# The order of VectorE's work in the up-projection of a hybrid encoder block

## The chip, the cores and the metric

The kernel runs on one core of a Trainium2 chip. The metric is the device time of one execution in microseconds. Five engines work side by side, each through its own list of instructions: TensorE (PE; its weight loads are PEld) multiplies matrices, VectorE (DVE), ScalarE (ACT) and GpSimd (POOL) work elementwise, and SyncE (SP) issues the DMAs between the chip's memory and the on-chip buffers. An instruction waits at the head of its engine's list until its inputs are there and its output's buffer is free, and everything behind it on that engine waits too.

## The reference

One encoder layer for 2048 frames of 1024 channels. The part that matters here is the second sub-layer:

```python
h2 = modulate(rms_norm(x, g_norm2[l]), shift2, scale2)
u = causal_depthwise_conv(h2 @ w_up[l], w_conv[l], b_conv[l])
val, gte = jnp.split(u, 2, axis=-1)
x = x + (1 + gate2[:, None, :]) * ((val * jax.nn.silu(gte)) @ w_down[l])
```

`w_up` is 1024 x 5632, so val and gte have 2816 columns each; the convolution over frames has three terms, from the frame itself and the two before it. All values are 32-bit floats.

## The kernel before

**Tiling.** The up-projection works through two halves of 1024 frames each, and in each half through 22 blocks of 128 columns of val with the same 128 of gte: `for n in range(2 * NF)`, 44 iterations, `half, f = divmod(n, NF)`. A product of 2 x 2 blocks is done with seven block products instead of eight (Strassen's scheme in Winograd's form), for which sums of the blocks are needed: of the inputs h2 (`h2[0]` to `h2[6]`), of the weights and of the results. Each 32-bit operand is split in two parts, a high one (a copy by ScalarE, L1185) and the rest (a subtraction by POOL or VectorE, L1186), and each block product is 4 x 3 matmuls with 128x512 results (`product`, L1257).

**An iteration.** The results lie in two tiles in TensorE's accumulators, `val` (v; halves a and b) and `gate` (g; halves c_ and d_). TensorE takes the products in a fixed order: 1 into b, 2 into d_, 3 into c_, product 0 of the following iteration into its a, then 4 into a, 5 into b, 6 into c_. Product 0 to 2 use the weight tiles `wua`, 3 to 6 `wub`. Between them VectorE adds (L1261): u2 = b + p1, where p1 is ScalarE's copy of a (L1457); b = d_ + u2, which is the row `v<-g,u` of the profile and is called v below; u3 = c_ + u2; and d_ = d_ + u3, the row `g<-g,u`, called g. ScalarE copies u3 into c_ (L1476), called the copy c. Products 4 and 5 write into v and so wait for v; product 6 waits for g.

**After the products.** `conv` forms the convolution: ScalarE writes the first term from v into cval (L1326, the tap), VectorE adds two more (L1334, L1336) and keeps the last two frames for the second half (halo, L1339); `gate_step` does the same with g into cgate, then silu on ScalarE (L1354) and the multiplication on VectorE (L1355). For an odd f, two blocks are then a pair, and four sums of their halves (gate sums, L1181 and L1366) go with the blocks to memory (`hid_s`, L1347) for the down-projection, which works in the same scheme. `gate_step` is a generator: its steps are done inside the next iteration (`before`).

**Weights.** `make_up` (first half) loads four weight blocks of the next iteration, forms four weight sums on VectorE (s1 = a21 + a22, s2 = s1 - a11, s3 = a11 - a21, s4 = a12 - s2, L1181), splits all seven and stores the sums (`wu_s`); `again_up` (second half) loads them from there. Both are generators too (`made`), stepped between the products. The tiles `ring` are a shared pool of 128x512 buffers for all loads and sums. In iterations 20 to 22 the splits of h2 for the second half come in as well (`swap`, `load_h2`; tiles `h_i_k` in an engine's order, `h` in the profile).

**What sets the order.** Inside the loop TensorE is held to the order of the program (`in_order(("PE",))`). The lists of the other engines are made by a scheduler, which takes from the program's instructions by its own costs and priorities, so there the program's order is one input among others.

Of the kernel before, what the change touches and what calls it, by code (L numbers as in the profile page):

```python
# [26 lines left out]
NF = DFF // P  # L27
# [20 lines left out]
def hybrid_block(ctx, tc, x, c, w_ada, b_ada, g1, w_in, w_fg2, b_fg2, g_gla, w_out, g2,  # L48
# [1124 lines left out]
    def raw(src):  # L1173
        t_ = ring.tile([P, CH], F, name="ring")
        if src is not None:
            dma.dma_start(out=t_ if len(src.shape) == 2 else t_.rearrange("p (k n) -> p k n", k=src.shape[1]), in_=src)
        return t_

    def combine(a, b, op):
        t_ = raw(None)  # L1180
        dve.tensor_tensor(out=t_, in0=a, in1=b, op=op)  # L1181
        return t_
# [17 lines left out]
    def up_block(f, i):  # L1200
        return w_upk[:, KH * (i % 2):KH * (i % 2) + KH, (NF * (i // 2) + f) * P:(NF * (i // 2) + f + 1) * P]

    def put_up(src, eng, res):
        res.append(parts(in_turn(wua if len(res) < 3 else wub[0], 6, [P, 2, CH], R), src, eng))

    def make_up(f, res):

        a11, a12, a21, a22 = (raw(up_block(f, i)) for i in range(4))

        def keep(i, t_):  # L1210
            dma.dma_start(out=wu_s[f][i], in_=t_)

        yield
        put_up(a11, pool, res)
        s1 = combine(a21, a22, ALU.add)
        s2 = combine(s1, a11, ALU.subtract)
        put_up(s2, pool, res)
        put_up(s1, pool, res)
        keep(0, s1)
        yield  # L1220
        s3 = combine(a11, a21, ALU.subtract)
        s4 = combine(a12, s2, ALU.subtract)
        keep(1, s2)
        put_up(s3, pool, res)
        keep(2, s3)
        yield
        put_up(a12, pool, res)
        yield
        put_up(s4, pool, res)
        keep(3, s4)  # L1230
        put_up(a22, pool, res)
        yield

    def again_up(f, res):

        a11, s2, s1 = raw(up_block(f, 0)), raw(wu_s[f][1]), raw(wu_s[f][0])
        yield
        put_up(a11, pool, res)
        s3, a12 = raw(wu_s[f][2]), raw(up_block(f, 1))
        put_up(s2, pool, res)  # L1240
        put_up(s1, pool, res)
        yield
        s4, a22 = raw(wu_s[f][3]), raw(up_block(f, 3))
        put_up(s3, pool, res)
        yield
        put_up(a12, pool, res)
        yield
        put_up(s4, pool, res)
        put_up(a22, pool, res)
        yield  # L1250
# [9 lines left out]
    def add(res, ps, other):  # L1260
        dve.tensor_tensor(out=res, in0=ps, in1=other, op=ALU.add)  # L1261
# [8 lines left out]
    for i in range(3):  # L1270
        for k in range(KH):
            load_h2(0, i, k, dve if (i + k) % 2 else pool)
        if i == 0:
            next(made)
    rest = []
    accs_o = iter([lambda: pools["o"].tile([P, CH], F, name="o"), lambda: ps_z.tile([P, CH], F, name="z"),
# [72 lines left out]
    def gate_step(half, f, cval, gate):  # L1349


        cgate = conv(NF + f, gate, "cgate", half)
        yield
        act.activation(out=cgate, in_=cgate, func=AF.Silu)  # L1354
        dve.tensor_tensor(out=cval, in0=cval, in1=cgate, op=ALU.mult)  # L1355
        q = f // 2
        if f % 2 == 0:
            store_hid(half, q, 0, cval[:, :CH])
            held_val[q] = cval
        else:  # L1360
            (a11, a21), (a12, a22) = ((t_[:, :CH], t_[:, CH:]) for t_ in (held_val.pop(q), cval))
            store_hid(half, q, 1, a12)
            store_hid(half, q, 2, a22)
            s1 = combine(a21, a22, ALU.add)
            s2 = combine(s1, a11, ALU.subtract)
            dve.tensor_tensor(out=a21, in0=a11, in1=a21, op=ALU.subtract)  # L1366
            s4 = combine(a12, s2, ALU.subtract)
            for o, t_ in ((3, s1), (4, s2), (5, a21), (6, s4)):
                store_hid(half, q, o, t_)
        yield  # L1370
# [64 lines left out]
    ordered.enter_context(in_order(("PE",)))  # L1435
    for n in range(2 * NF):
        half, f = divmod(n, NF)
        w, w_next = w_next, []
        s = n % 2
        val = val_next  # L1440
# [10 lines left out]
        def swap(i, now=None):  # L1451
            if half == 0 and (f == NF - 1 if now is None else now):
                for k in range(KH):
                    load_h2(1, i, k, pool if k % 2 else dve)
# [5 lines left out]
            halo_bias()  # L1460
        if n:
            product(b, 1, w, True)
        next(made, None)
        swap(1)
        next(before, None)
        product(d_, 2, w, True)
        add(u2, b, p1)
        next(made, None)
        swap(2)
        product(c_, 3, w, True)  # L1470
        next(made, None)
        swap(3)
        add(b, d_, u2)
        u3 = cv.tile([P, CH], F, name="u3", tag="p1", bufs=1)
        add(u3, c_, u2)
        act.activation(out=c_, in_=u3, func=AF.Copy)  # L1476
        add(d_, d_, u3)
        if n == 2 * NF - 1:
            next_down()
        if n + 1 < 2 * NF:  # L1480
            val_next = ps_u[2 * (1 - s)].tile([P, HT], F, name="v")
            product(val_next[:, 0:CH], 0, w_next, True)
            swap(0, f == NF - 2)
        next(made, None)
        product(a, 4, w, False)
        swap(4)
        if n == 2 * NF - 1:
# [12 lines left out]
        if n in MW:  # L1500
            make_wd(MW.index(n))
        before = gate_step(half, f, cval, gate)
    ordered.close()
    for _ in before:
        pass
# [179 lines left out]
```

## Time and profile before

| | us |
|---|---|
| median of 3 runs | 2674.64 |
| lowest, highest run | 2670.0, 2682.25 |
| profiled execution, its own time | 2680.58 |
| span of its trace | 2678.9 |
| PE busy | 2527.3 (94%) |
| DVE, ACT, POOL busy | 1704.7, 1321.9, 1284.0 |

The profiled execution lies at the upper end of the runs. The span is from the first to the last instruction of the trace. The up-projection's loop takes the span from about 1327 to 2231 us; the mean granted TensorE clock over the whole span is 0.984 of full speed. Busy shares of the whole span say little about one loop: TensorE is busy nearly everywhere, and what matters in the loop is for which other engine it waits.

### The profile page before, as it was taken

To read this page: it belongs to the slowest core of one execution; us is meant where nothing else is said; L and a number is where in the kernel's file an instruction comes from. 1 tells how busy PE (TensorE), PEld (TensorE's weight loads), DVE (VectorE), ACT (ScalarE), POOL (GpSimd) and SP (SyncE) were. 2 spreads that over 40 slices of the span, in tenths; PEclk is the share of its full clock that TensorE was granted. 3 is DMA by queue.
4 is the path that set the end of the run, shared out by engine and by line. 5 is a ranking of instruction groups with operands and counts; after the bars stand their busy time and mean duration, and the time that the engine had idled before them with its cause. 6 is when DMAs were issued, how large, how long until landed. Compare 5 with 4: busy or idle time off the path is not lost. (4 is left out here: it accounts for less than half of the span.)

```text
span 2678.9 us, 36699 instructions
## 1 busy us (share of the span) xinstructions
PE 2527.3 (94%) x12118; PEld 2066.3 (77%) x12118; DVE 1704.7 (64%) x2335; ACT 1321.9 (49%) x2416; POOL 1284.0 (48%) x1100
## 2 busy tenths in 40 slices
PE   5899999999899999999979999989999999999996
PEld 5788888888677777777768778778887877888885
DVE  6535652254988999999566666784554557454668
ACT  4523234232877788888434444454445444333343
POOL 2202122121755556776546556477556553252446
PEclk9999999999999999999989999999999999999998
DMA  8657954576855454554745555576556656544472
GB/s 286 191 173 249 290 170 141 154 241 185 266 185 170 129 149 147 160 164 127 240 139 184 189 174 183 162 243 224 196 174 204 205 181 233 164 142 130 165 273 77
DMA packets 420558, 499.47 MB, mean 186 GB/s; under 512 B 38270, under 2 KB 262796, under 8 KB 418320
## 3 DMA queue, kind: packets, MB, share of 16 engines
q1 hardware_dynamic: 420368, 497.12, 58.6%
q8 instruction: 96, 1.57, 0.3%
q14 instruction: 94, 0.77, 0.1%
HBM read 330.81 MB, written 166.20 MB: 186 GB/s over the span
## 5 line engine op out<-in xcount | busy, mean ns | idle before, releaser
L1009 POOL TENSOR_TENSOR bt<-bt,om 128x512 f32<-128x512 f32 (+2 forms) x320 | 314.2, 986 | 220.1 <-DVE om L1007 122.8
L1186 POOL TENSOR_TENSOR wub<-ring,wub 128x512 fp32r<-128x512 f32 x176 | 239.7, 1366 | 299.4 <-ACT wub L1185 296.7
L1257 PE MATMUL v<-h,wub 128*128 128x512 f32 x1056 | 259.3, 403 | 27.1 <-DVE v L1261 27.0
L1257 PE MATMUL v<-h,wua 128*128 128x512 f32 x1056 | 262.4, 397 | 8.5 <-POOL wua L1186 5.4
L1257 PEld LDWEIGHTS v<-h,wub 128*128 128x128 f32 x1056 | 204.1, 195 | 78.5 <-DVE v L1261 29.7
L1257 PE MATMUL g<-h,wub 128*128 128x512 f32 x1056 | 254.3, 390 | 0.0
L1007 DVE TENSOR_TENSOR_SCAN om<-sg,om,zero 128x513 f32<-128x513 f32 x189 | 240.5, 1272 | 16.0 <-ACT sg L1001 14.8
L1257 PEld LDWEIGHTS v<-h,wua 128*128 128x128 f32 x1056 | 200.9, 191 | 55.4 <-POOL wua L1186 6.6
L1257 PEld LDWEIGHTS g<-h,wub 128*128 128x128 f32 x1056 | 198.2, 188 | 41.9 <-DVE g L1261 0.3
L1651 PE MATMUL d<-h,wub 128*128 128x512 f32 x924 | 222.9, 391 | 0.0
L70 PE MATMUL tr<-ident,bt 128*128 128x128 f32 x1120 | 179.9, 277 | 37.8 <-DVE al L131 24.6
L1404 POOL TENSOR_TENSOR h<-h,h 128x512 fp32r<-128x512 f32 x77 | 116.5, 1516 | 194.7 <-ACT h L1403 173.4
L131 DVE TENSOR_TENSOR al<-tr,ah 128x512 fp32r<-128x512 f32 (+1 forms) x320 | 192.9, 603 | 19.4 <-ACT ah L130 18.6
L1186 POOL TENSOR_TENSOR wua<-ring,wua 128x512 fp32r<-128x512 f32 x132 | 192.1, 1467 | 24.5 <-ACT wua L1185 23.9
L287 POOL TENSOR_TENSOR wr<-wst,wr 128x1024 fp32r<-128x1024 f32 x28 | 71.0, 2540 | 275.0 <-ACT wr L286 275.0
L1651 PEld LDWEIGHTS d<-h,wub 128*128 128x128 f32 x924 | 173.5, 188 | 37.6
L1334 DVE SCALAR_TENSOR_TENSOR cval<-v,conv_w,cval 128x1023 f32<-128x1023 f32 x44 | 56.4, 1282 | 228.6 <-ACT cval L1326 220.0
L130 ACT ACTIVATE ah<-tr 128x512 fp32r<-128x512 f32 (+1 forms) x320 | 179.9, 562 | 26.2 <-PE tr L70 25.6
L70 PEld LDWEIGHTS tr<-ident,bt 128*128 128x128 f32 x1120 | 126.6, 140 | 85.0 <-DVE al L131 35.4
L1002 ACT ACTIVATE bt<-z 128x512 f32<-128x512 f32 (+2 forms) x320 | 174.0, 544 | 0.0
L401 PE MATMUL mm<-wr,hh 128*128 128x512 f32 (+1 forms) x448 | 170.0, 379 | 3.3 <-DVE vt L131 2.0
L403 PE MATMUL mm<-wr,hl 128*128 128x512 f32 (+1 forms) x448 | 168.2, 375 | 0.0
(311 smaller groups left out, 5995.7 us busy)
## 6 DMA issues: line engine op xcount, KB each, us to landing
ring<-in_w_up_dram SPq DMA_DIRECT2D x154, 256.0 KB, 4.9
ring<-hid_s SPq DMA_DIRECT2D x154, 256.0 KB, 4.3
wst<-in_w_in_dram SPq DMA_DIRECT2D x45, 512.0 KB, 7.5
wu_s<-ring SPq DMA_DIRECT2D x88, 256.0 KB, 2.4
hid_s<-cval SPq DMA_DIRECT2D x88, 256.0 KB, 2.4
ring<-wu_s SPq DMA_DIRECT2D x88, 256.0 KB, 5.1
kt<-k_hl SPq DMA_DIRECT2D x80, 256.0 KB, 3.2
vt<-v_hl SPq DMA_DIRECT2D x80, 256.0 KB, 3.3
```

What stands on the lines that cost most here:

```text
L70: pe.transpose(out=o, in_=i, identity=ident)
L130: act.activation(out=hi, in_=ps, func=AF.Copy)
L131: dve.tensor_tensor(out=lo, in0=ps, in1=f32(hi), op=ALU.subtract)
L401: pe.matmul(out=ps[:, :n], lhsT=hh[:, k, sl], rhs=wh, start=k == 0, stop=False)
L403: pe.matmul(out=ps[:, :n], lhsT=hl[:, k, sl], rhs=wh, start=False, stop=k == KD - 1)
L1002: act.activation(out=b1, in_=z[:, :w], func=AF.Sigmoid, scale=0.125)
L1007: dve.tensor_tensor_scan(out=om[:, 0:n_][:, ::-1], data0=beta[:, 0:n_][:, ::-1], data1=zero[0][:, 0:1].broadcast_to([P, n_]), initial=firs ...
L1009: pool.tensor_tensor(out=b1, in0=b1, in1=om[:, 1:w + 1], op=ALU.mult)
L1186: eng.tensor_tensor(out=t_[:, 1], in0=src, in1=f32(t_[:, 0]), op=ALU.subtract)
L1257: pe.matmul(out=ps, lhsT=lhsT, rhs=rhs, start=begin and k == 0 and m == 0, stop=k == KH - 1 and m == 2, skip_group_check=not begin)
L1404: pin(eng.tensor_tensor(out=t_[:, 1], in0=src, in1=f32(t_[:, 0]), op=ALU.subtract))
L1651: pin(pe.matmul(out=ps, lhsT=hd[:, l_, tsl], rhs=w[:, r_], start=begin and q == 0 and m == 0, stop=q == NQ2 - 1 and m == 2, skip_group_che ...
```

## The change

Three things are altered, all in the up-projection. VectorE is held to the order of the program, too, in iterations 2 to 19 and 24 to 43 (`ordered_v`). The program's order is rewritten: v is added ahead of product 3, the generators' steps are cut anew, so that in each iteration they come in turns, with `gate_step` split ahead of and behind the multiplication, and a weight sum s1 ahead of it. And `make_up` stores each weight sum where it is made. No instruction is added or taken away. L1355, L1366, L1457 and L1476 of before are L1356, L1368, L1462 and L1481 in the changed kernel.

```diff
@@ make_up
         put_up(a11, pool, res)
         s1 = combine(a21, a22, ALU.add)
+        keep(0, s1)
+        yield
         s2 = combine(s1, a11, ALU.subtract)
+        keep(1, s2)
         put_up(s2, pool, res)
         put_up(s1, pool, res)
-        keep(0, s1)
         yield
         s3 = combine(a11, a21, ALU.subtract)
+        keep(2, s3)
+        put_up(s3, pool, res)
+        put_up(a12, pool, res)
+        yield
         s4 = combine(a12, s2, ALU.subtract)
-        keep(1, s2)
-        put_up(s3, pool, res)
-        keep(2, s3)
-        yield
-        put_up(a12, pool, res)
-        yield
+        keep(3, s4)
         put_up(s4, pool, res)
-        keep(3, s4)
         put_up(a22, pool, res)
         yield
@@ again_up
         put_up(a11, pool, res)
+        yield
         s3, a12 = raw(wu_s[f][2]), raw(up_block(f, 1))
         put_up(s2, pool, res)
         put_up(s1, pool, res)
         yield
         s4, a22 = raw(wu_s[f][3]), raw(up_block(f, 3))
         put_up(s3, pool, res)
-        yield
         put_up(a12, pool, res)
@@ ahead of the loop
-        if i == 0:
+        if i < 2:
             next(made)
@@ gate_step
         act.activation(out=cgate, in_=cgate, func=AF.Silu)
+        yield
         dve.tensor_tensor(out=cval, in0=cval, in1=cgate, op=ALU.mult)
+        yield
         q = f // 2
@@ the loop
     for n in range(2 * NF):
         half, f = divmod(n, NF)
+        ordered_v = ExitStack()
+        if 2 <= n < NF - 2 or n >= NF + 2:
+            ordered_v.enter_context(in_order(("DVE",)))
...
         if n:
             product(b, 1, w, True)
+        next(before, None)
         next(made, None)
+        next(before, None)
         swap(1)
-        next(before, None)
         product(d_, 2, w, True)
         add(u2, b, p1)
+        add(b, d_, u2)
         next(made, None)
         swap(2)
         product(c_, 3, w, True)
-        next(made, None)
         swap(3)
-        add(b, d_, u2)
         u3 = cv.tile([P, CH], F, name="u3", tag="p1", bufs=1)
         add(u3, c_, u2)
         act.activation(out=c_, in_=u3, func=AF.Copy)
         add(d_, d_, u3)
+        next(made, None)
...
         next(made, None)
+        next(before, None)
         product(a, 4, w, False)
...
         before = gate_step(half, f, cval, gate)
+        ordered_v.close()
```

**VectorE in iteration 16**, an even one of the first half. `ring<-ring` are weight sums, `ring<-cval`, `ring<-ring,cval`, `cval<-cval` and `ring<-cval,ring` the gate sums, `u_16718<-v,p_16717` is u2 and the second u is u3. Before:

```order
L1334 SCALAR_TENSOR_TENSOR cgate<-g,conv_w,cgate 128x1023
L1261 TENSOR_TENSOR u_16718<-v,p_16717 128x512
L1336 SCALAR_TENSOR_TENSOR cgate<-g,conv_w,cgate 128x1022
L1339 COPY halo<-g 128x2
L1355 TENSOR_TENSOR cval<-cval,cgate 128x1024
L1181 TENSOR_TENSOR ring<-cval 128x512
L1181 TENSOR_TENSOR ring<-ring,cval 128x512
L1366 TENSOR_TENSOR cval<-cval 128x512
L1261 TENSOR_TENSOR v<-g,u_16718 128x512
L1261 TENSOR_TENSOR u_16804<-g,u_16718 128x512
L1181 TENSOR_TENSOR ring<-cval,ring 128x512
L1181 TENSOR_TENSOR ring<-ring 128x512 x2
```

VectorE in the same iteration of the changed kernel, from the end of its convolution:

```order
L1339 COPY halo<-g 128x2
L1181 TENSOR_TENSOR ring<-ring 128x512
L1356 TENSOR_TENSOR cval<-cval,cgate 128x1024
L1261 TENSOR_TENSOR u_16718<-v,p_16717 128x512
L1261 TENSOR_TENSOR v<-g,u_16718 128x512
L1181 TENSOR_TENSOR ring<-ring 128x512
L1261 TENSOR_TENSOR u_16780<-g,u_16718 128x512
L1261 TENSOR_TENSOR g<-g,u_16780 128x512
L1181 TENSOR_TENSOR ring<-ring 128x512 x2
L1181 TENSOR_TENSOR ring<-cval 128x512
L1181 TENSOR_TENSOR ring<-ring,cval 128x512
L1368 TENSOR_TENSOR cval<-cval 128x512
```

The four gate sums went from ahead of v and u3 to behind g; the weight sum s1 came ahead of the multiplication, and u2 behind it.

**SyncE in the second half**, at the stores of the pair q = 7 (iteration 38; `wu_s_3_201` is s4 of a following iteration, `in_w_up_dram` a weight block, `wd_s` are sums for the down-projection). Before:

```order
L1347 DMA hid_s_0_119<-cval 128x512
L1176 DMA ring<-in_w_up_dram 128x4x128
L1382 DMA wd_s_127<-ring 128x512
L1382 DMA wd_s_129<-ring 128x512
L1347 DMA hid_s_1_120<-cval 128x512
L1347 DMA hid_s_2_121<-cval 128x512
L1347 DMA hid_s_3_122<-ring 128x512
L1347 DMA hid_s_4_123<-ring 128x512
L1176 DMA ring<-wu_s_3_201 128x512
L1347 DMA hid_s_5_124<-cval 128x512
L1347 DMA hid_s_6_125<-ring 128x512
L1176 DMA ring<-in_w_up_dram 128x4x128 x2
```

SyncE at the same pair in the changed kernel:

```order
L1347 DMA hid_s_0_119<-cval 128x512
L1176 DMA ring<-in_w_up_dram 128x4x128
L1176 DMA ring<-wu_s_3_201 128x512
L1176 DMA ring<-in_w_up_dram 128x4x128
L1384 DMA wd_s_127<-ring 128x512
L1384 DMA wd_s_129<-ring 128x512
L1347 DMA hid_s_1_120<-cval 128x512
L1347 DMA hid_s_2_121<-cval 128x512
L1347 DMA hid_s_3_122<-ring 128x512
L1347 DMA hid_s_4_123<-ring 128x512
L1176 DMA ring<-in_w_up_dram 128x4x128
L1347 DMA hid_s_5_124<-cval 128x512
```

The loads of s4 and of one weight block moved ahead of the stores of the gate sums.

**ScalarE in iteration 21**, where VectorE is not held to the program's order. `h_i_k` are copies of h2 for the second half, `p_17795` is p1 of iteration 22. Before:

```order
L1185 ACTIVATE h_1_2_17575<-ring 128x512
L1354 ACTIVATE cgate<-cgate 128x1024
L1185 ACTIVATE h_1_3_17580<-ring 128x512
L1185 ACTIVATE h_2_0_17608<-ring 128x512
L1185 ACTIVATE wub_17681<-ring 128x512
L1185 ACTIVATE h_2_1_17613<-ring 128x512
L1185 ACTIVATE h_2_2_17618<-ring 128x512
L1476 ACTIVATE g<-u_17664 128x512
L1185 ACTIVATE h_2_3_17623<-ring 128x512
L1185 ACTIVATE h_3_0_17643<-ring 128x512
L1457 ACTIVATE p_17795<-v 128x512
```

ScalarE at the same place in the changed kernel:

```order
L1185 ACTIVATE h_2_1_17606<-ring 128x512
L1185 ACTIVATE h_2_2_17611<-ring 128x512
L1185 ACTIVATE h_2_3_17616<-ring 128x512
L1354 ACTIVATE cgate<-cgate 128x1024
L1185 ACTIVATE h_3_0_17633<-ring 128x512
L1185 ACTIVATE h_3_1_17638<-ring 128x512
L1185 ACTIVATE h_3_2_17643<-ring 128x512
L1185 ACTIVATE h_3_3_17648<-ring 128x512
L1185 ACTIVATE wub_17680<-ring 128x512
L1481 ACTIVATE g<-u_17653 128x512
L1462 ACTIVATE p_17795<-v 128x512
```

silu moved behind the copies h_1_3 and h_2_0 to h_2_3, and the copy c behind h_3_0 to h_3_3 and a weight copy.

## Rows read from the trace of the kernel before

**Rows 1.** Busy table of line L1257's instructions by stretch of the loop, TensorE.

```profile
core 0: us, PE busy (x) PEld busy (x), PEclk, DMA share, GB/s
1630.39:1649.54 19.15, 19.15 (x86) 15.77 (x85) 1.00 0.50 165
1327.14:1391.95 64.81, 44.91 (x169) 35.01 (x168) 0.82 0.51 158
1391.95:1749.68 357.73, 349.20 (x1514) 285.44 (x1513) 0.99 0.55 180
1749.68:1820.12 70.44, 62.68 (x253) 50.25 (x252) 0.93 0.75 244
1839.27:2210.84 371.57, 366.09 (x1597) 298.92 (x1596) 1.00 0.59 194
2210.84:2231.14 20.30, 18.47 (x73) 14.39 (x71) 0.92 0.46 153
```

**Rows 2.** PE's waits, 1324 to 2231: total us, times, longest us.

```profile
PE v L1257 <- DVE v L1261: 27.0, 15, 4.4
...
PE v L1257 <- POOL wua L1186: 5.4, 2, 3.0
PE v L1257 <- ACT wua L1185: 3.1, 1, 3.1
```

**Rows 3.** Timeline of PE, iteration 16: start, us, instruction [idle before <- releaser].

```profile
1682.36 7.32 PE L1257 MATMUL v<-h,wub 128*128 128x512 f32 x24 [2.54 <-DVE v L1261]
```

**Rows 4.** Timeline of DVE, iteration 16.

```profile
1668.53 1.14 DVE L1181 TENSOR_TENSOR ring<-ring 128x512 f32<-128x512 f32 x1 [1.82 <-DMA t_s<-ring]
1671.47 1.28 DVE L1334 SCALAR_TENSOR_TENSOR cval<-v,conv_w,cval 128x1023 f32<-128x1023 f32 x1 [1.79 <-ACT cval L1326]
...
1678.30 1.23 DVE L1355 TENSOR_TENSOR cval<-cval,cgate 128x1024 f32<-128x1024 f32 x1 [1.12 <-ACT cgate L1354]
1679.61 0.69 DVE L1181 TENSOR_TENSOR ring<-cval 128x512 f32<-128x512 f32 x1
...
1681.61 0.69 DVE L1261 TENSOR_TENSOR v<-g,u 128x512 f32<-128x512 f32 x1
```

**Rows 5.** Timeline of ACT, iteration 16.

```profile
1669.71 0.63 ACT L1185 ACTIVATE wua<-ring 128x512 fp32r<-128x512 f32 x1 [1.81 <-DVE ring L1181]
1670.24 1.19 ACT L1326 ACTIVATE cval<-v,conv_b,conv_w 128x1024 f32<-128x1024 f32 x1
```

**Rows 6.** Timeline of ACT, iteration 33.

```profile
2013.67 0.63 ACT L1185 ACTIVATE wub<-ring 128x512 fp32r<-128x512 f32 x1 [3.76 <-DMA ring<-in_w_up_dram]
...
2014.95 1.19 ACT L1326 ACTIVATE cval<-v,conv_b,conv_w 128x1022 f32<-128x1022 f32 x1
...
2022.45 0.63 ACT L1185 ACTIVATE wua<-ring 128x512 fp32r<-128x512 f32 x1 [2.17 <-DMA ring<-in_w_up_dram]
```

**Rows 7.** Line L1181, 1391 to 2211: count, duration ns min/median/max.

```profile
L1181 DVE TENSOR_TENSOR ring<-ring x74: 674/692/1794, 1403.1 to 1764.9; 128x512 f32<-128x512 f32 x74
```

**Rows 8.** Timeline of ACT ahead of iteration 14.

```profile
1627.87 1.21 ACT L1326 ACTIVATE cval<-v,conv_b,conv_w 128x1024 f32<-128x1024 f32 x1 [0.76 <-PE v L1257]
```

**Rows 9.** Timeline of DVE, iteration 21.

```profile
1778.58 3.53 DVE L1186 TENSOR_TENSOR h<-ring,h 128x512 fp32r<-128x512 f32 x2
...
1784.25 0.69 DVE L1261 TENSOR_TENSOR v<-g,u 128x512 f32<-128x512 f32 x1
```

**Rows 10.** Timeline of POOL, iterations 21 and 22.

```profile
1793.81 11.26 POOL L1186 TENSOR_TENSOR h<-ring,h 128x512 fp32r<-128x512 f32 x7
```

**Rows 11.** Timeline of DVE, iteration 0.

```profile
1357.58 0.69 DVE L1261 TENSOR_TENSOR u<-v,p 128x512 f32<-128x512 f32 x1 [1.92 <-ACT p L1457]
...
1361.99 0.69 DVE L1181 TENSOR_TENSOR ring<-ring 128x512 f32<-128x512 f32 x1 [2.40 <-DMA ring<-in_w_up_dram]
...
1363.20 4.09 DVE L1181 TENSOR_TENSOR ring<-ring 128x512 f32<-128x512 f32 x3
```

**Rows 12.** Timeline of PE, iterations 0 and 1.

```profile
1366.10 2.88 PE L1257 MATMUL g<-h,wub 128*128 128x512 f32 x12
...
1382.03 7.37 PE L1257 MATMUL v<-h,wub 128*128 128x512 f32 x24 [2.07 <-DVE v L1261]
```

More of the change, by code (lines that the diff above doesn't have):

```diff
@@ L1215, in make_up @@
         s1 = combine(a21, a22, ALU.add)
+        keep(0, s1)
+        yield
         s2 = combine(s1, a11, ALU.subtract)
+        keep(1, s2)
         put_up(s2, pool, res)
         put_up(s1, pool, res)
-        keep(0, s1)
         yield
         s3 = combine(a11, a21, ALU.subtract)
-        s4 = combine(a12, s2, ALU.subtract)
-        keep(1, s2)
+        keep(2, s3)
         put_up(s3, pool, res)
-        keep(2, s3)
-        yield
         put_up(a12, pool, res)
         yield
+        s4 = combine(a12, s2, ALU.subtract)
+        keep(3, s4)
         put_up(s4, pool, res)
-        keep(3, s4)
         put_up(a22, pool, res)
```

## The prediction

> **What bounds the kernel now.** I read the table of stretches first [rows 1]. An iteration in which nothing waits takes 19.15 us, and TensorE is busy for all of it at the full clock: seven products, of 2.74 us each. So the up-projection can only gain what its 44 iterations take above that. Dividing the stretches: iterations 2 to 19 take 357.73 us where 18 x 19.15 = 344.70 would do, so 13.0 are lost; 20 to 22 take 70.44 instead of 57.45, 13.0 lost; 24 to 42 take 371.57 instead of 363.85, 7.7 lost; 0 and 1 take 64.81 instead of 38.30, 26.5 lost; the last, which has six products, 20.30 instead of 16.42, 3.9 lost. Together 64 of 2680.58 us.
>
> Next, what ended these waits [rows 2]: of 35.5 us of waiting in the products, 27.0 in 15 waits are `v <- DVE v L1261`, VectorE's sum b + d + u2, on which product 4 starts. The other two rows belong to iteration 0, and one wait, the longest on POOL, to iteration 22. Where a wait is long, the granted clock is lower as well: 0.99 in iterations 2 to 19, 0.93 in 20 to 22, and 1.00 in 24 to 42, whose waits are under 2 us [rows 1]. So a long wait costs more than its own length.
>
> Then one such wait, iteration 16 (it begins at 1668.68). On PE, product 4 starts at 1682.36 after 2.54 idle [rows 3], so its inputs from TensorE were ready at 1679.82. VectorE finished v at 1681.61 + 0.69 = 1682.30 [rows 4]. Going back on VectorE: three sums of gate products stand in front of v (1679.61 to 1681.61, 2.0 us); the multiplication before them waited for ScalarE's silu; the whole chain began late, at 1671.47, because the tap (the first term of the convolution, on ScalarE) began at 1670.24. The tap stood behind a weight copy which at 1669.71 waited 1.81 us for a weight sum [rows 5], and this sum ran on VectorE at 1668.53, as early as the scheduler could put it, after 1.82 us of waiting for a DMA [rows 4]. From the tap's start to v's end it is 1682.30 - 1670.24 = 12.06 us. v is due 11.1 us after the iteration's start, so any tap later than about 0.95 us ahead of the start makes PE wait.
>
> The second half of the loop has no weight sums; there the tap is late for a load. In iteration 33 (from 2013.68) a weight copy waited 3.76 us for in_w_up and the tap came at 2014.95, 1.27 after the start; later another copy, waiting 2.17 us for a load, stood ahead of silu [rows 6].
>
> **The change part by part.** No instruction is added or removed; all is order.
>
> *Gate sums behind v (even iterations of both halves, as far as VectorE is held to program order).* Three sums leave the path to v: 0.69 + 0.69 + 0.68 by their rows, 2.0 us by their starts [rows 4]. The u2 sum, 0.68, moves from between the convolution's steps to behind the multiplication and is neutral. One weight sum, s1, comes ahead of the multiplication, but there VectorE sat idle 1.12 us waiting for silu [rows 4], and a sum takes 0.69 in the median [rows 7]: it is hidden, and costs up to 0.7 if stretched to its worst, 1.794. So the tap-to-v time falls to 10.0 us and tolerates a tap up to 1.1 us after the start.
>
> *Weight sums in program order.* Their copies on ScalarE then stand behind the tap and silu instead of ahead of them, so the tap no longer waits for sums. In an undisturbed iteration the tap begins 2.5 us ahead of the start (14: 1627.87 for 1630.39) [rows 8]; from there v is ready 3.5 us early. Even if every tap stayed as late as now, iteration 16 would end v at 1680.30 instead of 1682.30 and wait 0.5. The gate sums and the last weight sums now follow g. Product 3 ends 8.2 us after the start, and u3, the copy c and g, some 0.7 each, bring g to 10.3; six sums of 0.69 bring VectorE to 14.5, and the next convolution begins 1.2 us after its tap [rows 4, 5], at 19.15 - 2.5 + 1.2 = 17.9: covered by 3.4 us.
>
> *The second half.* Three sums leave the path in its even iterations, where nothing was lost anyway; in the odd ones silu stands ahead of the copies that wait for loads, which takes about 0.6 off iteration 33, the copy's own 0.63 (its wait for the load ran beside VectorE's convolution) [rows 6]. The larger part is SyncE: s4's and a22's loads are issued ahead of the stores of the gate sums and not behind them. How much earlier they land no row shows. The bounds are 0, if something else than the stores holds the loads, and 3.76, the whole wait [rows 6]. I take 1.5, nearer the lower, which puts iteration 33's tap where the shorter chain no longer makes PE wait; with nothing from it, 3 of the 7.7 us would remain.
>
> Sum for iterations 2 to 19 and 24 to 42: 13.0 + 7.7 lost now, 2 left (bounds 1 and 4, or 9 if a new wait of 0.5 us came in every second iteration): **-19**.
>
> *Iterations 20 to 22, where VectorE stays with the scheduler.* There v moves ahead of the multiplication in all three. Iteration 20 has the same three sums ahead of v and loses that part. In 21 v ran at 1784.25, behind two splits of h (3.53 us, stretched) and the multiplication [rows 9]; one more split of up to 1.8 and no multiplication stand ahead of it now, so v comes some 2 us earlier; but silu goes behind eight copies of h, and the copy c behind three more, so that the last product of the iteration may wait up to 2 us for g. In 22 PE waits 3.05 us for POOL's first split of a11, behind seven splits of h (11.26 us) [rows 2, 10]; one of these, 1.6 us, now goes behind it: about 1.4 remains. I leave 2.5 in iteration 21, 2.5 in 22 (wait and clock) and 1.5 for a late tap in 20 or 21: 13.0 becomes 6.5, **-6.5** (from -11 to +4).
>
> *The start and the end.* In iteration 0 the copy p no longer stands behind a weight copy; VectorE waited 1.92 us for it at u2, and up to that is taken off PE's longest wait, of 4.4 us [rows 2, 11]. But u3 and g now follow four weight sums, the first of which waits for its load until 1361.99 [rows 11]. These take 4 x 0.69 = 2.8 us at least, and 4.8 by the row of three (4.09) plus 0.69; u3, the copy c and g add 2, so g ends at 1366.8 to 1368.8. Product 6 needs it; it began at 1366.10 [rows 12] and would now begin 1.9 earlier, at 1364.2: a new wait of 2.6 to 4.6 against the 1.9 won, +0.7 to +2.7. Iteration 1 loses the sums ahead of its v, which stands ahead of the multiplication; the wait for v there was 2.07 us [rows 12], and with the lower clock behind it up to 4.0 are gone. A long new wait in 0 lowers the clock as well, so I take 0 for the two: bounds -4 and +4. Iteration 43 has the same sums in another order: 0.
>
> Total: -19 - 6.5 = -25.5 us on the profiled execution of 2680.58, so 2655; the profiled run lies 5.9 us above the median of the runs, so against 2674.64 it is **2649**. A measurement of this kernel can tell about 0.5% from no change, 13 us.
>
> **A rule against it.** The sums that read two SBUF tensors take 0.674 us at best, 0.692 in the median and 1.794 at worst [rows 7]; the long ones lie beside POOL's splits. The addition that reads PSUM took 0.69 in iteration 16 and in 21, where POOL was busy [rows 4, 9]. The Trainium skill, SBUF — State Buffer, section Who interferes with whom, says that a VectorE instruction with two SBUF inputs and a GpSimd instruction reading SBUF exclude each other for the whole instruction; the trace agrees with it, by the 1.794 against 0.674. By that rule the gathered sums would each wait for a split.
>
> **The rivals.** *Port:* six sums in a row, each at 1.79 instead of 0.69, end 6.6 us later, at 21 us instead of 14.5, which is past the next convolution's 17.9 by 3.2. With v now 3.5 us early that costs nothing in most iterations; where the tap was late anyway, up to 1 us in each of 18: -7 in all, 2668. For it speaks the maximum, against it the median. *The waits keep their place:* the loads set the tap, not the sums, and the loads come no earlier, or stand behind gate stores that now come 3 us later; half of both gains goes: -13, 2662. For it speak iterations of the second half, which have no sums and are late all the same. *The turn gives back:* silu and c behind copies of h, and g late in 21 and 22, so that 20 to 22 lose 19 instead of 13: -19 + 6 = -13, 2662. *Slower:* VectorE in program order waits at s1, ahead of the multiplication, u2 and v. If the loads of a21 and a22 come later than 7.8 us after the iteration's start (s1, multiplication, u2 and v take 3.3 us together, of 11.1), PE waits for the rest. At 2.5 us too late in each of 18 iterations 45 us are lost where 13 are now, less the 5.7 and 6.5 of the other stretches: +20, 2694. Against it: in iteration 16 a sum of this kind ran at 1668.53, before the iteration began [rows 4], 8 us ahead of that point. That the order isn't what the change says can be ruled out: it is read off above.
>
> **How the numbers follow.** Forecast 2649 (2640 to 2660): 0.60. Waits keep their place, 2662: 0.17. Turn gives back, 2662: 0.08. Port, 2668: 0.08. Slower, 2694: 0.07. Up to 2667 this holds over 0.8, so the range is 2640 to 2667. 0.5% faster lies at 2661.3: the forecast with a part of the cases around 2662 gives 0.67; within 0.5% 0.26; slower 0.07.
>
> **What would show it.** Right: waits `v <- DVE v` of under 2 us in all in iterations 2 to 19 and 24 to 42, stretches of about 345 and 366 us, gate sums behind g, the tap ahead of the iteration's start. In 20 to 22 about 64 us. Wrong: VectorE idle before a weight sum for a DMA, with PE waiting behind it; iterations of the second half that keep their late taps; `g <- DVE g` as a new wait in iterations 0, 21 or 22.

## The result

The changed kernel takes 2864.07 us in the median of 6 runs (2860.17 to 2868.32), the kernel before 2680.05 in as many; the ratio is 1.0674, 95% interval 1.0644 to 1.0704. It is slower by 184 us where some 25 us less were forecast, and lies far outside the range.

TensorE's waits in the loop of the changed kernel tell where (engine, line, what it waited for: us, times, longest), to be read beside [rows 2]:

```profile
PE g L1257 <- DVE v L1261: 153.9, 44, 15.5
PE tr L70 <- DVE ht L894: 9.1, 1, 9.1
```

All the waits of [rows 2] are gone, those for v before product 4 too. In their place there is one kind: a product into the gate's tile g waits for v, 44 times, once in every iteration. The products that write g with `wub` weights are 3 and 6. Iteration 16 (it begins at 1726.63) shows which one, and how. TensorE and then VectorE, as in [rows 3, 4]:

```profile
1729.39 2.88 PE L1257 MATMUL g<-h,wua 128*128 128x512 f32 x12
1734.55 4.61 PE L1257 MATMUL g<-h,wub 128*128 128x512 f32 x12 [2.28 <-DVE v L1261]
```

```profile
1725.50 1.28 DVE L1334 SCALAR_TENSOR_TENSOR cval<-v,conv_w,cval 128x1023 f32<-128x1023 f32 x1 [6.33 <-ACT cval L1326]
...
1730.66 1.09 DVE L1181 TENSOR_TENSOR ring<-ring 128x512 f32<-128x512 f32 x1
1731.87 1.23 DVE L1356 TENSOR_TENSOR cval<-cval,cgate 128x1024 f32<-128x1024 f32 x1
1733.01 0.68 DVE L1261 TENSOR_TENSOR u<-v,p 128x512 f32<-128x512 f32 x1
1733.80 0.70 DVE L1261 TENSOR_TENSOR v<-g,u 128x512 f32<-128x512 f32 x1
...
1739.20 0.69 DVE L1261 TENSOR_TENSOR u<-g,u 128x512 f32<-128x512 f32 x1 [4.11 <-PE g L1257]
```

Product 2 begins at 1729.39. Product 3 begins at 1734.55, in the moment in which v ends (1733.80 + 0.70 = 1734.50), and ran slowly (4.61 us where 2.88 is the usual row; the granted clock over it was 0.63). VectorE itself is on its plan: the tap is early, s1 runs while ScalarE does silu, and v ends 7.87 us after the iteration's start, where the prediction's steps give about 7.6. But TensorE now needs it 5.5 us after the start and no longer at 11. So VectorE waits for product 3 afterwards (4.11 us before u3), and TensorE and VectorE take turns.

The table of stretches, to be read beside [rows 1] (us, PE busy, PEld busy, clock, DMA): iterations 0 and 1, 2 to 19, 20 to 22, 24 to 42, and 43:

```profile
1328.58:1397.34 68.76, 41.51 (x169) 33.43 (x168) 0.80 0.47 143
1397.34:1819.02 421.68, 372.20 (x1513) 299.24 (x1512) 0.94 0.46 152
1819.02:1896.30 77.28, 63.79 (x253) 51.16 (x252) 0.89 0.74 238
1916.52:2390.85 474.33, 403.17 (x1598) 323.20 (x1597) 0.91 0.45 151
2390.85:2412.05 21.20, 18.44 (x73) 14.38 (x71) 0.92 0.41 145
```

The stretches held to VectorE's order, 421.68 and 474.33 us instead of 357.73 and 371.57, hold 167 of the 181 us between the two spans. Only part of it is waiting: the products' waits grew from 35.5 to 153.9, by 118; PE's busy time in the five stretches grew by 58 (899.1 instead of 841.4), the same matmuls at a granted clock of 0.94 and 0.91 in the two long stretches instead of 0.99 and 1.00; and the wait in tr, transposes that lie between products in iteration 0, grew by 3.

### The profile page after: what moved, and what is told of

The parts are those of the page before. It is cut to its first block, busy times and chain, and to the rows that moved or that the text cites. A ratio compares the mean times of both kernels' runs of the same rounds, so it can differ in the third digit from the quotient of the medians.

```text
span 2859.9 us, 36776 instructions
## 1 busy us (share of the span) xinstructions
PE 2586.6 (90%) x12118; PEld 2105.2 (74%) x12118; DVE 1718.6 (60%) x2335; ACT 1330.4 (47%) x2416; POOL 1285.0 (45%) x1100
## 5 line engine op out<-in xcount | busy, mean ns | idle before, releaser
L1257 PE MATMUL g<-h,wub 128*128 128x512 f32 x1056 | 324.0, 467 | 153.9 <-DVE v L1261 153.9
L1257 PEld LDWEIGHTS g<-h,wub 128*128 128x128 f32 x1056 | 239.2, 231 | 226.5 <-DVE v L1261 108.4
L1257 PE MATMUL v<-h,wua 128*128 128x512 f32 x1056 | 259.0, 394 | 0.0
L1257 PE MATMUL v<-h,wub 128*128 128x512 f32 x1056 | 247.4, 390 | 0.0
L1257 PEld LDWEIGHTS v<-h,wua 128*128 128x128 f32 x1056 | 202.5, 192 | 46.6
L1186 POOL TENSOR_TENSOR wua<-ring,wua 128x512 fp32r<-128x512 f32 x132 | 185.3, 1412 | 106.3 <-ACT wua L1185 100.0
L1257 PEld LDWEIGHTS v<-h,wub 128*128 128x128 f32 x1056 | 198.7, 188 | 41.8
L70 PE MATMUL tr<-ident,bt 128*128 128x128 f32 x1120 | 180.2, 277 | 38.1 <-DVE al L131 24.4
L1185 ACT ACTIVATE wub<-ring 128x512 fp32r<-128x512 f32 x176 | 109.0, 630 | 221.2 <-PE g L1257 127.0
L70 PEld LDWEIGHTS tr<-ident,bt 128*128 128x128 f32 x1120 | 126.7, 140 | 85.6 <-DVE al L131 35.5
```

Source lines behind the costliest of these rows:

```text
L70: pe.transpose(out=o, in_=i, identity=ident)
L1185: act.activation(out=t_[:, 0], in_=src, func=AF.Copy)
L1186: eng.tensor_tensor(out=t_[:, 1], in0=src, in1=f32(t_[:, 0]), op=ALU.subtract)
L1257: pe.matmul(out=ps, lhsT=lhsT, rhs=rhs, start=begin and k == 0 and m == 0, stop=k == KH - 1 and m == 2, skip_group_check=not begin)
```

## The experiments

Each ratio below is against executions of the kernel before that were timed beside that run; their medians lie between 2673.91 and 2678.64 us.

**The theory and its rivals.** c_ and d_ are the two halves of one tile, g. v = b + d_ + u2 reads d_, product 3 writes c_. In the changed program v stands ahead of product 3. The theory: for that reason, and since readers and writers are ordered by tile and not by half, product 3 waits until v has read; before, v stood behind product 3 in the program and the products went on. The programs' lists of instructions, each with what it waits for, fit. The first rows of product 3 in iteration 16, in the changed kernel and then before (in brackets the engines' counts that an instruction waits for; DVE is VectorE's, and the value that is waited for in the changed kernel is the one that the addition v counts up to):

```
L1257 MATMUL g_16708<-h2_3_0_14098,wub4_16622 128x512 [waits DVE_49]
L1257 MATMUL g_16708<-h2_3_0_14098,wub4_16622 128x512
L1257 MATMUL g_16708<-h2_3_0_14098,wub4_16622 128x512 [waits Pool_49]
```

```
L1257 MATMUL g_16708<-h2_3_0_14097,wub4_16607 128x512 x2
L1257 MATMUL g_16708<-h2_3_0_14097,wub4_16607 128x512 [waits Pool_49]
```

The rival: VectorE's list in program order is too slow, whoever waits for it.

**One line put back.** The changed kernel with v behind product 3 again:

```diff
         add(u2, b, p1)
-        add(b, d_, u2)
...
         swap(3)
+        add(b, d_, u2)
         u3 = cv.tile([P, CH], F, name="u3", tag="p1", bufs=1)
```

> The changed kernel with one line put back: v = b + d_ + u2 is added behind product 3 in the program again, and everything else stays as changed. Theory A (product 3 waits for v since v reads the other half of the tile that product 3 writes, and v stood ahead of it in the program; 153.9 us in 44 waits): these waits are gone, v is waited for by product 4 only, and the time is near what was predicted, 2640 to 2665. Theory B (VectorE in program order is itself too slow a list, whoever waits for it): product 4 waits in place of product 3 by several us per iteration, and the time stays over 2750.

Measured: 2655.62 us, ratio 0.9914 (0.9889 to 0.9939). One line is worth 208 us, and the rest of the change makes the kernel faster by 0.9%. The same five stretches in this run:

```profile
1328.01:1390.31 62.30, 44.45 (x169) 34.90 (x168) 0.81 0.50 156
1390.31:1736.35 346.04, 345.45 (x1514) 283.56 (x1513) 1.00 0.56 184
1736.35:1807.03 70.68, 62.22 (x253) 50.14 (x252) 0.93 0.73 244
1826.47:2190.32 363.85, 363.85 (x1598) 299.50 (x1596) 1.00 0.59 197
2190.32:2207.95 17.63, 16.83 (x73) 13.25 (x71) 1.00 0.52 178
```

Where VectorE is held to the order hardly anything is left to win: 363.85 us for 19 iterations is 19.15 each, and 346.04 for 18 is 1.3 more than that. The rival falls.

**That line alone.** The kernel before with v ahead of product 3 and nothing else changed:

```diff
         add(u2, b, p1)
+        add(b, d_, u2)
...
         swap(3)
-        add(b, d_, u2)
```

> The kernel before with that one line alone: v is added ahead of product 3 in the program; VectorE stays with the scheduler, the generators as before. Theory A: product 3 waits for v in each of 44 iterations, at least 1 us (the addition and its way) and up to 5, plus the lower clock: 2800 to 2930. Theory B: within 20 us of the kernel before.

Measured: 2746.18 us, ratio 1.0251 (1.0225 to 1.0277). The line does it alone, but less than expected: the scheduler now takes v as early as it can. TensorE's waits, and one iteration in which v was as early as can be, VectorE and then TensorE:

```profile
PE g L1257 <- DVE v L1261: 84.9, 44, 15.2
```

```profile
1624.28 0.70 DVE L1261 TENSOR_TENSOR v<-g,u 128x512 f32<-128x512 f32 x1 [0.77 <-PE g L1257]
```

```profile
1625.04 3.01 PE L1257 MATMUL g<-h,wub 128*128 128x512 f32 x12 [0.79 <-DVE v L1261]
```

Again 44 waits. VectorE stood idle for 0.77 us until product 2 was done, added at once, and TensorE still lost 0.79 and, over the whole iteration, 1.1 us. That is the floor of such an order: product 3 can't begin before product 2 has ended and v has been added. The changed kernel is slower than this one; by its rows of iteration 16 the reason is that its program order puts the multiplication and u2 ahead of v (there v began 1.5 us after product 2's end, at 1732.27), but no run takes that alone.

**The tile as the cause.** The changed kernel, order untouched, with c_ and d_ as two tiles; the terms of cgate then take two instructions of 512 columns each instead of one:

```diff
-        gate = ps_u[2 * s + 1].tile([P, HT], F, name="g")
-        a, b, c_, d_ = val[:, 0:CH], val[:, CH:], gate[:, 0:CH], gate[:, CH:]
+        gate = tuple(ps_u[2 * s + 1].tile([P, CH], F, name=nm) for nm in ("gc", "gd"))
+        a, b = val[:, 0:CH], val[:, CH:]
+        c_, d_ = (t_[:, :] for t_ in gate)
```

> The changed kernel with the gate's two halves c_ and d_ in two tiles of one bank each instead of one of two; the terms of the gate's convolution are formed in two instructions each (512 columns), some 0.3 us more of VectorE and ScalarE per iteration. The order stays the changed one. Theory A with the wait put down to the shared tile: product 3 no longer waits for v, 2645 to 2670. Rival (the wait is for the numbers that product 3 needs, or for VectorE's pace): 2840 to 2870 as changed.

Measured: 2655.62 us, ratio 0.9923 (0.9897 to 0.9949). The numbers that product 3 needs and VectorE's order are as in the changed kernel, and the 153.9 us are gone; its waits for v lie before product 4 again:

```profile
PE v L1257 <- DVE v L1261: 13.8, 11, 4.4
```

VectorE is no earlier than it was: in iteration 16 product 3 (into c_, here `gc`) begins 3.4 us before v is added from d_ (`gd`), and in iterations 1 to 42 it is ahead of v in every one.

```profile
1661.57 2.89 PE L1257 MATMUL gc<-h,wub 128*128 128x512 f32 x12
```

```profile
1665.01 0.70 DVE L1261 TENSOR_TENSOR v<-gd,u 128x512 f32<-128x512 f32 x1
```

So product 3 waited only for the tile. The control, the kernel before with the same split:

> The kernel before with the gate's halves in two tiles, as the control of the run with the changed order: what the split of the convolution costs or gives by itself. Theory A: nothing waited for the gate's tile there, so within 15 us of the kernel before (2665 to 2695). Rival: the shared tile cost something in the kernel before as well, and it becomes faster by over 15 us.

Measured: 2670.12 us, 0.9972 (0.9941 to 1.0003), no difference that can be told, though its ten executions spread from 2653 to 2693.

**The other tile.** If that is so, product 4 waits for v for the same reason: it writes a, and v is added into b, the other half of one tile. So now `val` as two tiles, with g as one again (the terms of cval in two instructions each): first in the run with one line put back, then in the kernel before, without any change of order.

```diff
-            val_next = ps_u[2 * (1 - s)].tile([P, HT], F, name="v")
-            product(val_next[:, 0:CH], 0, w_next, True)
+            val_next = tuple(ps_u[2 * (1 - s)].tile([P, CH], F, name=nm) for nm in ("va", "vb"))
+            product(val_next[0][:, :], 0, w_next, True)
```

> The run with v behind product 3, with v's tile (a and b) as two tiles of one bank each. Theory: product 4 writes a and waits for the sum into b only because they share a tile; split, product 5 is the first that waits, 2.74 us later. So the wait in iteration 0 falls from 5.2 to 2.4, in 20 from 3.3 to 0.6, in 21 from 5.2 to 2.5, with some of the lower clock: 2642 to 2650. Rival: the products wait as before (the wait is for numbers or the same bank), or v's convolution in two instructions each costs as much: 2653 to 2662.

Measured: 2648.28 us, ratio 0.9883 (0.9822 to 0.9944), the lowest median of this study; the interval overlaps that of the run without the split (0.9889 to 0.9939). Waits, and then the stretches 2 to 19, 20 to 22, and 24 to 42:

```profile
PE vb L1257 <- DVE vb L1261: 4.4, 3, 2.0
...
PE g L1257 <- DVE g L1261: 2.3, 2, 2.2
```

```profile
1382.01:1726.65 344.64, 344.64 (x1514) 283.83 (x1512) 1.00 0.56 184
1726.65:1797.60 70.95, 62.70 (x253) 49.06 (x252) 0.95 0.72 239
1816.80:2180.59 363.79, 363.79 (x1598) 299.62 (x1597) 1.00 0.60 196
```

No product 4 waits for v; product 5 does, 3 times. In the ordered stretches not a microsecond is lost. The number came out as the theory said, but only half by its way. In iteration 0, where the wait had been 4.4 and not 5.2, 2.8 us were won, and 1.4 in iterations 2 to 19 and 1.1 in the last. In 20 and 21 the waits for v fell to 0.6 and 2.0 as said, but 20 to 22 together take 70.95 instead of 70.68, with new waits for g in them (2.3 in all) and one for v in 22. And 5.6 us of the difference between the two traces lie ahead of the up-projection's first product, where nothing was altered.

> The kernel before with v's halves in two tiles and no other edit. By the same theory the 15 waits for v (27.0 us, 14 of them under 2.8) move to product 5 and nearly vanish, without any change of the order by hand: 2676 - 25 - some clock, 2640 to 2655. Rival: with the split convolution the scheduler makes other lists, as in the control with the gate's tile split, whose waits lay elsewhere (4.6 to 6.6 us in five iterations of the second half) and whose runs spread from 2653 to 2693: 2660 to 2690.

Measured: 2660.24 us, 0.9906 (0.9876 to 0.9936): without moving a line of the program, some 18 us, as much as the hand-made order with v in its place gives. That is at the edge of the rival's range, and both have a part in it. In the first half the tile is the cause: v is late in iteration 16 there too (it ends 12.1 us after the start), but product 4 (into `va`) begins ahead of it and nothing waits:

```profile
PE vb L1257 <- DVE vb L1261: 4.7, 5, 2.1
```

```profile
1668.68 2.90 PE L1257 MATMUL va<-h,wub 128*128 128x512 f32 x12
```

```profile
1669.07 0.69 DVE L1261 TENSOR_TENSOR vb<-g,u 128x512 f32<-128x512 f32 x1
```

Iterations 2 to 19 lose 4.1 us instead of 13.0. In 24 to 42 nothing is lost instead of 7.7, but there v itself ends by 10.9 us after the start where it took up to 12.8 before: with the convolution in two pieces the scheduler made other lists, and that half of the gain can't be put down to the tile. Both tiles split under the changed order:

> The changed kernel, its order untouched (v added ahead of product 3), with v's and the gate's halves in two tiles each. Theory: neither product 3 nor product 4 waits for the sum v any more, so the order as changed costs nothing: at or below the run with v's tile split and v behind product 3 (2648), 2640 to 2652. Rival: VectorE's and ScalarE's further instructions (the convolutions in two pieces each) make v or g late for products 5 and 6: 2653 to 2670.

Measured: 2659.78 us, 0.9949 (0.9928 to 0.9970). This lies in the rival's range, though the theory holds for the tiles: products 3 and 4 wait for v no more, and in the ordered stretches 1.3 us are lost in all. But iterations 20 to 22 lose 16.6; product 0 waits there for weights (5.9 us in all), product 5 for v (2.6) and product 6 for the copy c (2.2).

**What the order is worth.** The run with one line put back, without VectorE's program order (`pass` for `enter_context`):

> The run with v behind product 3, without VectorE's program order in any iteration; the generators' new cuts stay. It tells what the order by hand is worth. Theory A (the order is what takes gate sums and weight sums out of the path to v): the waits of the kernel before come back, 2668 to 2685. Rival (the new cuts of the generators are enough for the scheduler): 2650 to 2662.

Measured: 2682.47 us, 1.0001 (0.9971 to 1.0031). All of the gain is gone, and in iterations 2 to 19 product 4 waits for v again:

```profile
PE v L1257 <- DVE v L1261: 16.0, 5, 4.7
```

They aren't the waits of the kernel before: there iterations 4, 8, 12 and 16 lost most (1.7 to 4.4 us), here 5, 9, 13 and 17 (3.3 to 7.5), which have no gate sums. With the new cuts alone the scheduler gains nothing. What the gate sums cost by themselves the next run tells. **With the gate sums ahead of u2 and v again**, under program order. All four stand there; before, three of them stood ahead of v, and the fourth behind u3:

```diff
         next(made, None)
         next(before, None)
+        next(before, None)
         swap(1)
...
         next(made, None)
-        next(before, None)
         product(a, 4, w, False)
```

> The run with v behind product 3 (2655.6), with the four gate sums put back ahead of u2 and v, VectorE still in program order. Theory (the three sums ahead of v were the last part of the late chain): in the first half's even iterations v ended 9.8 us after the start in that run, due at 11.0; four sums of 0.69 bring it to 12.5, a wait of 1.5 in each of 9 iterations and a part of it in the second half's: 2666 to 2680. Rival (the late tap alone made the waits, and it is early now): 2654 to 2660.

Measured: 2768.26 us, 1.0340 (1.0303 to 1.0378). The time is far beyond the expectation. In the first half it is as expected in kind: 355.42 instead of 346.04 us for iterations 2 to 19, with 1.1 to 1.7 us lost in each even one and none in the odd ones. In the second half, iterations 24 to 42, it loses 109 us, nearly all in the odd ones, which have no gate sums at all:

```profile
1385.96:1741.38 355.42, 347.30 (x1514) 283.25 (x1513) 1.00 0.55 180
1831.24:2304.10 472.86, 390.37 (x1597) 313.77 (x1596) 0.91 0.47 155
```

VectorE in iteration 29, and POOL beside it:

```profile
1961.43 9.73 DVE L1356 TENSOR_TENSOR cval<-cval,cgate 128x1024 f32<-128x1024 f32 x1 [1.56 <-ACT cgate L1354]
```

```profile
1960.17 1.33 POOL L1186 TENSOR_TENSOR wub<-ring,wub 128x512 fp32r<-128x512 f32 x1
1961.44 1.31 POOL L1382 TENSOR_TENSOR ring<-ring 128x512 f32<-128x512 f32 x1
1962.70 3.72 POOL L1186 TENSOR_TENSOR wua<-ring,wua 128x512 fp32r<-128x512 f32 x3
1966.37 1.27 POOL L1382 TENSOR_TENSOR ring<-ring 128x512 f32<-128x512 f32 x1
1967.59 1.27 POOL L1186 TENSOR_TENSOR wub<-ring,wub 128x512 fp32r<-128x512 f32 x1
1968.81 1.27 POOL L1382 TENSOR_TENSOR ring<-ring 128x512 f32<-128x512 f32 x1
```

The multiplication, 1.23 us where nothing meets it, takes 9.73. POOL was in a row of instructions without a gap, 16 of them from 1950.12 on, when it began; seven more followed the one that ran then, until 1970.08, and the multiplication ended 1.1 us later, about its own length. It is the same in all nine odd iterations (8.6 to 9.9 us). A row of POOL's beside it isn't enough for that: in the kernel before the multiplication meets such rows in the same iterations and takes at most 1.84 us (last section). What differs was not followed: the loads' place on SyncE changed with the sums', and a weight copy ahead of silu waits for a load again (2.06 us), as in [rows 6], but no run takes that alone.

**The turn** from the first half to the second, iterations 20 to 22. With one line put back they still take 70.68 us, where 70.44 were before. The order there, too:

```diff
-        if 2 <= n < NF - 2 or n >= NF + 2:
+        if n >= 2:
```

> The run with v behind product 3 (2655.6), with VectorE in program order in iterations 20 to 23 too. In that run iterations 20 and 21 still lose 5.2 and 8.1 us (v late by 3.3 and 5.2). Theory A (there the scheduler's list puts weight sums and splits of h ahead of v, program order would not): 2645 to 2652. Rival (in program order the splits of h stand ahead of u2 and v and wait for loads that can only begin when a product is done): the turn loses 10 us more than now, 2665 to 2680.

Measured: 2661.77 us, 0.9926 (0.9898 to 0.9954). Iteration 20 loses nothing now (5.2 without the order), but 21 waits 14.0 us at once for v. VectorE there, from 1756.74:

```profile
1770.06 1.68 DVE L1356 TENSOR_TENSOR cval<-cval,cgate 128x1024 f32<-128x1024 f32 x1 [3.50 <-ACT cgate L1354]
1771.66 3.43 DVE L1186 TENSOR_TENSOR h<-ring,h 128x512 fp32r<-128x512 f32 x2
1775.01 0.68 DVE L1261 TENSOR_TENSOR u<-v,p 128x512 f32<-128x512 f32 x1
1775.62 6.18 DVE L1186 TENSOR_TENSOR h<-ring,h 128x512 fp32r<-128x512 f32 x4
1781.71 0.69 DVE L1261 TENSOR_TENSOR v<-g,u 128x512 f32<-128x512 f32 x1
```

Six splits of h stand ahead of v, and silu is late (the multiplication waits 3.50 us for it): the order that the rival named, though VectorE waits for no load between them. The time lies in neither range: 21 loses 17.0 us where 8.1 were lost and 22 loses 1.7, but 20 wins 5.2, so the turn is longer by 5.5 us and not by 10. Last, the fastest kernel with the order in iteration 20 alone added (`n < NF - 1`):

> The fastest run so far (v behind product 3, v in two tiles, 2648.3) with VectorE's program order in iteration 20 as well. With the order in 20 to 23, iteration 20 lost nothing and 21 lost 17.0; with the scheduler in 20 to 23, 20 lost 5.2 and 21 8.1. Theory (20 gains by the order, and only the splits of h in 21 suffer from it): 20 loses nothing, 21 and 22 as in the run without it, 2642 to 2646. Rival (what 20 no longer loses, 21 loses, since the splits of h and the weights wait for the same loads): 2647 to 2653.

Measured: 2658.60 us, 0.9942 (0.9922 to 0.9961). That is beyond both ranges. Iteration 20 loses nothing (4.9 without the order) and 21 as much as without it (4.7 and 4.2), but 22 loses 14.2 where 4.4 were lost, on product 0 of the following iteration, which waits for the weights (the longest of each row; the others belong to iteration 0):

```profile
PE va L1257 <- ACT wua L1185: 10.4, 2, 7.3
PE va L1257 <- POOL wua L1186: 6.2, 2, 3.9
```

So neither of the two orders mends the turn: what one iteration gains a later one gives back. What would carry weights and h2 through it together stays open.

## Why the prediction was wrong, and where it was right

- **What bounds the kernel**: right for most of the loop. Waits for v were 27.0 of the 35.5 us of waiting. The kernel before with v in two tiles has 4.7 us of them left, and the loop loses some 39 us where it lost 64; most of these 39 lie in iterations 0 and 20 to 22.
- **The step that failed** is the first sentence of the change's part, that all is order, and with it that v stays due 11.1 us after the iteration's start. The text followed v on VectorE, and never asked what its place in the program does to TensorE, whose own order hadn't moved. By moving ahead of product 3 the reader of d_ became something that product 3, which writes the other half of the same tile, waits for: v was due 5.5 us after the start, and 44 waits of 153.9 us in all were the price, a term that the sum doesn't have. The price would have stood in the same working: v ends some 7.6 us after the start by the prediction's own steps, product 2 ends at 5.5; 2.1 us in each iteration whose tap is in time and more in the others, over 90 us in 44, and then a lower clock, as [rows 1] had shown it for the stretches with the longer waits. None of the rivals held it: the one on the slow side looked for a late load.
- **Gate sums and weight sums out of the path**: right, and by its amount, once v stands behind product 3. With the line put back, 1.3 and 0.0 us are lost where 2 were forecast to be left of 20.7. The run without program order shows that the order does it, and the run with the gate sums ahead of v that these cost 1.1 to 1.7 us in each even iteration of the first half. What the weight sums' place is worth by itself no run takes.
- **The second half's loads**: right in kind, too small in size. In iteration 33 of the run with the line put back the tap began at 1996.66, 2.2 us ahead of the start at 1998.85; before, 1.27 behind [rows 6]. So the tap won 3.5 us and not 1.5, near the upper bound of 3.76. The copy ahead of the tap there waits for a load again, but for 1.83 us instead of 3.76; how much of the 3.5 is SyncE's order and how much ScalarE's list no run takes apart.
- **Iterations 20 to 22**: of the 6.5 us nothing came. With the line put back, 13.2 are lost there and 13.0 before. But the scheduler's lists there are not the changed kernel's, from which the term was read: in 20 and 21 the multiplication stands ahead of v again. The run with the gate in two tiles, whose program has v in its changed place, loses 10.4. With the line put back, iteration 22 loses nothing now; but 20 loses 5.2 (2.8 before) and 21 loses 8.1 (4.2). In 20 a weight sum stood on VectorE for 3.88 us beside three of POOL's instructions, 3.2 more than its own length, about as long as PE's wait for v there (3.25):

```profile
1738.63 3.88 DVE L1181 TENSOR_TENSOR ring<-ring 128x512 f32<-128x512 f32 x1 [0.89 <-DMA ring<-in_w_up_dram]
```

```profile
1738.15 1.29 POOL L1382 TENSOR_TENSOR ring<-ring 128x512 f32<-128x512 f32 x1
1739.40 1.31 POOL L1186 TENSOR_TENSOR wub<-ring,wub 128x512 fp32r<-128x512 f32 x1
1740.66 1.30 POOL L1382 TENSOR_TENSOR ring<-ring 128x512 f32<-128x512 f32 x1
```

- **The start and the end**: iteration 1 lost its wait, as said. Iterations 0 and 1 took 62.30 us with the line put back instead of 64.81, within the bounds, but not for the reasons given: u3 of iteration 0 ran ahead of the four weight sums there (at 1359.81), not behind them as in the changed kernel (1367.25). The last took 17.63 instead of 20.30, where 0 was forecast.
- **The total** without the failed step: 2655.62 measured against 2649 forecast, and by the stretches 24.4 us less against 25.5. That this is so near is in part luck: the 6.5 us that the turn didn't give were made up by the start and the end (2.5 and 2.7), for which 0 was forecast.
- **The port rival** was right on the length of some sums and wrong on the cost. In the run with the line put back the last two gate sums take 1.8 us each in iterations 2 to 19 (in 24 to 42 they take 0.69):

```profile
L1181 DVE TENSOR_TENSOR ring<-cval,ring 128x512 f32<-128x512 f32 x9 | 16.2, 1797 | 0.0
L1368 DVE TENSOR_TENSOR cval<-cval 128x512 f32<-128x512 f32 x9 | 16.2, 1795 | 0.0
```

They end 18.7 us after the start in iteration 16, and the next convolution begins at 20.0, after 1.3 us of waiting for ScalarE: the cover holds, by 1.3 us and not by 3.4.

## What to carry to other kernels

When an instruction moves in the program, look at what it reads and writes, and at every engine that writes the same tile behind it, not only at its own engine's list: the rows that didn't move may have got a new wait. Two halves of one tile are one thing to the ordering in this kernel; giving them a tile each took away the wait that the change made, and in the first half most of those that it was meant to remove. And hold an order by hand only where the instructions it holds are ready in that order: the same order that freed iterations 2 to 19 made one wait of 14 us in iteration 21, where splits of h stood ahead of v.

## What was not expected of the hardware

VectorE's multiplication of two on-chip tensors can be held not for one POOL instruction but for the rest of a row of them: 9.73 us in the run with the gate sums ahead, and 3.88 for a sum beside three of POOL's in the run with the line put back, where 1.23 and 0.69 are their own lengths. The prediction had taken 1.79, the longest of [rows 7], for the worst.

It is not always so. In the kernel before the same multiplication also meets a row of 10 to 13 of POOL's instructions without a gap, in each odd iteration from 25 to 41, and yet takes 1.22 to 1.84 us. In iteration 27 it began within the first of these two instructions of POOL's and got its turn when that one had ended; the second then took 2.29 us instead of 1.3:

```profile
1906.80 1.75 DVE L1355 TENSOR_TENSOR cval<-cval,cgate 128x1024 f32<-128x1024 f32 x1 [1.76 <-ACT cgate L1354]
```

```profile
1906.16 1.30 POOL L1380 TENSOR_TENSOR ring<-ring 128x512 f32<-128x512 f32 x1
1907.41 2.29 POOL L1186 TENSOR_TENSOR wua<-ring,wua 128x512 fp32r<-128x512 f32 x1
```

What decides whether VectorE gets its turn within a row isn't shown by any run here. The Trainium skill, SBUF — State Buffer, section Who interferes with whom, says that a VectorE instruction with two SBUF inputs contends with a GpSimd instruction that reads SBUF, and that the ports they share are an exclusive lock. The trace agrees that one waits for the other, and shows further that the wait can be longer than one instruction. The convolution's instructions, which read the accumulators and one on-chip tensor, kept their 1.28 us in iterations 24 to 42 of the kernel before and of the run with the gate sums ahead.
